# A sixth weight buffer, receptance written in place, and the first unit's small products spread among dense steps

## The chip, the cores and the metric

The kernel runs on one core of one Trainium2 chip. The metric is the device time of one execution in microseconds. It was timed three times before the change: 1114.33, 1113.28 and 1114.30, median 1114.3.

## The reference, cut to what matters

The model has two layers, batch 1, 256 positions, width 2048, all in 32-bit floats. The first layer is an RWKV-7 mixer, the second a sparse attention mixer; only the first is touched here. Its core, cut:

```python
rkvz = jnp.einsum('nbtd,nde->nbte', mixed[:4], w_rkvz)        # four 2048 x 2048 products
decay = jnp.exp(-jnp.exp(w_log))
a = jax.nn.sigmoid(a0 + (xa @ a1) @ a2)
kk = heads(k * k_k); kk = kk / max(norm(kk), 1e-12)
k = k * (1.0 + (a - 1.0) * k_a)
o = wkv7_scan(r, decay, k, v, -kk, kk * a)                      # 32 heads of 64
o = group_norm(o) * ln_g + ln_b
bonus = jnp.sum(r * k * r_k, axis=-1, keepdims=True) * v
y = ((o + bonus) * jax.nn.silu(z)) @ w_o
```

The scan updates a 64 x 64 state per head and position: `S = S*w + (S a) b + v k`, and reads `o = S r`.

## The kernel before, in words

**Dense products.** Every weight is read once from memory in raw pieces of [128, 1024] floats by the SP queue (class `Weights`, `load`, L172). ScalarE copies a unit of a piece to a rounded high part (`whi`, L207), VectorE subtracts to get the low part (`wlo`, L192). TensorE then makes three matmuls where one would do: high by high, high by low, low by high. Raw buffers are five (`RAWB`), units are split three ahead of use (`AHEAD`). `ensure` (L194) asks for the piece that lies as many pieces on as there are raw buffers each time it splits a unit.

**Stages.** The value rows come first, then z and k columns in turn (`stage_k`, L715, works out decay, normalised keys and the rest for each block of 128 columns and stores them as `sp` in memory, `spd`). A triangular inverse for each chunk of 64 positions is worked out on VectorE (`stage_t`, L810), for the first half of the heads early, for the second half during the scan. The scan works in chunks of 64 positions, four of them, and in eight units of four heads (two column blocks `x`, two heads `h` each).

**The scan.** From there on the order on every engine is written out by hand (`in_order`). The receptance columns of unit U+1 and later the output product are a stream of dense steps, each of three matmuls of 256 columns (`pair_block`, L1248; L1257 to L1259), which `fill(n)` (L1273) places n at a time between the small matmuls of the scan. After each dense step `sch.pump()` lets the background work (`stage_t`) put its next instruction into VectorE's program. Preparing a unit has these steps in `prep` (L1049): `G` and `Y` complete the inverse, `B0`, `B1` transpose, `A0`, `A1` make the receptance-key products (each 48 matmuls of 64 x 64 on four chunks), `M0` to `M2` mask them on VectorE. `scale_r` (L1031) multiplies the receptance by the decay into `ar` and makes `mb`, the receptance times the bonus keys. Unit 0 is prepared by the list `PROLOGUE`, later units by `AUX`, a table of steps by phase.

A unit then runs twelve phases (`phase`, L1107): for each of four chunks a removal (`L1105`), a solve (`L1128`) and an output and state update (`L1134`, `L1137`). Phase number v is 3 times the chunk plus the step. In phase 0 the 32 matmuls of the bonus sums (`L1116`) come first. `FILL` gives the number of dense steps behind each phase: 32 a unit, as many as a unit of receptance has. The prologue has 16 of them.

`SPL` holds a unit's `sp`: keys and their inverse-decayed partner (512 columns), decays (260), bonus keys `kr` (256), decayed negative keys `at` (256), and behind these 256 more for the receptance that `scale_r` writes.

Of the kernel before, what the change touches and what calls it, by code (L numbers as in the profile page):

```python
# [71 lines left out]
KLAG = 2  # L72
AUX = {2: ("B0",), 3: ("G",), 4: ("B1", "Y"), 7: ("A0",), 9: ("A1",), 10: ("T", "M2"), 11: ("M0", "M1")}
NORM = {0: ("s0", "s1"), 1: ("s2", "s3", "rg"), 2: ("v",), 3: ("b",), 4: ("nmr",), 5: ("02", "24"), 6: ("46",), 7: ("68",), 8: ("g", "+", "z")}
FILLL = (3, 4, 4, 0, 0, 5, 4, 0, 4, 0, 4, 4)
PROLOGUE = ("R0", "R1", 6, "G", "B0", 4, "I", "Y", "B1", 2, "A0", 2, "A1", "M2", "M0", "M1", "V5", 2)
ZHOOK = 9
PACES, PACE, HOLD = (0.0, 1.8, 0.9, 0.9), [0.0], [False]
FILL = (3, 4, 4, 0, 0, 5, 4, 0, 4, 0, 4, 4)
FILLO, LASTFILL = 4, 36  # L80
QZ = (0, 25, 24, 1, 2, 23, 22, 21, 3, 20, 19, 18, 4, 17, 16, 15, 14, 13, 12, 11, 10)
# [63 lines left out]
class Weights:  # L145


    def __init__(self, tc, pool, raw_bufs, ahead):
        self.tc = tc
        self.nc, self.pool, self.raw_bufs, self.ahead = tc.nc, pool, raw_bufs, ahead  # L150
        self.pieces, self.order, self.loads, self.raw, self.hl = [], [], [], {}, []
        self.loaded = self.split = self.taken = 0
        self.on_pool = set()
        self.kept_from, self.kept_pool = math.inf, None
        self.due, self.late, self.hold = [], False, False

    def add(self, ap, per, queue=True):
# [14 lines left out]
    def load(self, n):  # L172
        while self.loaded < min(n, len(self.loads)):
            p = self.loads[self.loaded]
            ap, per = self.pieces[p]
            n_, cols = ap.shape[1:]
            t = self.raw_pool.tile([128, 1024], F32, name="wraw", bufs=self.raw_bufs)
            v = t[:, :n_ * cols].rearrange("p (k c) -> p k c", k=n_)
            self.nc.sync.dma_start(v, ap)
            self.raw[p] = [v, n_ // per]  # L180
            self.loaded += 1
# [12 lines left out]
    def ensure(self, n):  # L194
        while self.split < min(n, len(self.order)):
            p, u = self.order[self.split]
            if not self.hold:
                self.low()
            self.load(self.loads.index(p) + self.raw_bufs)
            ap, per = self.pieces[p]  # L200
# [18 lines left out]
def hybrid_kernel(ctx: ExitStack, tc: tile.TileContext, a: dict, out: bass.AP):  # L219
# [475 lines left out]
    ph0.release()  # L695
    banks(acc=(2, 0, 1), la=(3,), rn=(4, 7), ab=(5, 6))
    late = tc.alloc_tile_pool(name="late", bufs=1, side="right")
    kph = tc.alloc_tile_pool(name="kph", bufs=1)
# [16 lines left out]
    def stage_k(j):  # L715
# [16 lines left out]
        ksb = tmp("ksb")  # L732
        sqk = tmp("t1")
        S.activation(ksb, pk, AF.Copy)
# [16 lines left out]
        yield 1000.0  # L751
        rnx = tmp("rnx")
        S.activation(rnx.rearrange("p (a b n) -> p a b n", a=2, b=2),
# [12 lines left out]
        yield 800.0  # L766
        nk = tmp("nk")
        V.scalar_tensor_tensor(nk, ksb, KKN[:, j:j + 1], rn[:, :256], op0=OP.mult, op1=OP.mult)
# [166 lines left out]
    def phase_z3():  # L935
        nonlocal A10, T00, vt, zt
        ps = two()
        for k in range(NK):
            yield from rows_step(ps, "z", k, W.get(), 512)
            used.add(("z", k))  # L940
            if k == ZHOOK:
                sch.require(lambda: len(a1done) == 16)
                kph.release()
                early = tc.alloc_tile_pool(name="early", bufs=1, side="right", reuse_waits="tile")
                early_pool.append(early)
                one = lambda name, shape: early.tile(shape, F32, name=name)
                SPL0.extend(one(f"spl0{x}", [128, SPW + 256]) for x in range(2))
# [28 lines left out]
    one = lambda name, shape: scan.tile(shape, F32, name=name)  # L976
    SPL = [SPL0, [one(f"spl1{x}", [128, SPW + 256]) for x in range(2)]]
    Yb.append(one("Yb1", [128, 2, NCH, 64]))
# [45 lines left out]
    def parts(U, x):  # L1024
# [3 lines left out]
                t[:, SPW - 512:SPW - 256],  # L1028
                t[:, SPW - 256:].rearrange("p (x c t) -> p x c t", x=2, c=NCH))

    def scale_r(U, x):  # L1031
# [3 lines left out]
        pr = rps[U % 2][:, 256 * x:256 * x + 256]  # L1035
        V.tensor_tensor(ar[:, 1], c3(pr), pp[:, :, 1:], op=OP.mult)
        V.tensor_tensor(mb[:, x], pr, kr, op=OP.mult)
        G.tensor_copy(PCH[U][:, x], pp[:, :, CH])

# [9 lines left out]
    def prep(step, U):  # L1049
# [19 lines left out]
        elif step[0] == "B":  # L1069
# [6 lines left out]
            sch.t += 300  # L1076
        elif step[0] == "A":
            x = int(step[1])
            if x == 0:
                AT[U] = (pair_tile(2), rps[U % 2])  # L1080
            both, m = AT[U]
            BK, pp, kr, ar = parts(U, x)
            for c in range(NCH):
                o = x * 256 + c * 64
                for e in range(2):
                    for h in range(2):
                        k = h ^ e
                        PE.matmul(both[R[k], h * 512 + o:h * 512 + o + 64], BK[R[h], c, k, :], ar[R[h], 1, c, :], start=True, **mm)
                for h in range(2):
                    PE.matmul(m[R[h], o:o + 64], BK[R[h], c, h, :], ar[R[h], 0, c, :], start=True, **mm)  # L1090
            sch.t += 900
        else:
# [14 lines left out]
    def phase(U, c, p):  # L1107
        uv, px, pu, pS = UV[U % 2], view(U, 0, 64), view(U, 64, 64), view(U, 128, 64)
        O = view(U, 192 + 64 * c, 64)
        st = SST[U][0] if c else None  # L1110
        if p == 0:
            if c == 0:
                for i in range(NCH):
                    for x, h in each:
                        o = x * 512 + 448 + 2 * i
                        PE.matmul(PBK[U][H(x, h), o:o + 2], mb[R[h], x, 64 * i:64 * i + 64], ones2[R[h]], start=True, **mm)  # L1116
            removal(U, c)
            if c:
                for k, o in enumerate((px, O)):
                    for x, h in each:  # L1120
                        PE.matmul(o[H(x, h), x], ARS[U % 2][x][R[h], k, c - 1, :], st[R[h], x, :], start=False, **mm)
            X = scan.tile([128, 2, 64], F32, name="X", bufs=2)
# [139 lines left out]
    def stream():  # L1262
        for u in range(NU):
            yield from pair_block("r", rps[u % 2])
        phase_done.add("r")
        banks(acc=(0, 1))
        for nb, k0, k1 in OSEQ:
# [48 lines left out]
    for U in range(NU):  # L1316
# [3 lines left out]
        for v in range(12):  # L1320
# [23 lines left out]
            if v == 6 and U + 1 < NU:  # L1344
                scale_r(U + 1, 0)
                scale_r(U + 1, 1)
            for step in AUX.get(v, ()):
                if step == "T":
                    if U:
                        turn_y(P)  # L1350
                elif U + 1 < NU:
                    prep(step, U + 1)
            if U:
# [15 lines left out]
            if v == 10:  # L1369
                load_rows(vt, vd, U)  # L1370
                load_rows(zt, zd, U)
            fill(FILLO if U + 1 == NU else FILLL[v] if U + 2 == NU else FILL[v])
            sch.pump()
# [22 lines left out]
    def open_kv():  # L1396
        nonlocal bp, kvp, xlp, ssh, rsh
        scan.release()
        early_pool[0].release()
        late.release()  # L1400
        bp = ctx.enter_context(tc.tile_pool(name="bp", bufs=1, side="right"))
        kvp = tc.alloc_tile_pool(name="kvp", bufs=1)
# [513 lines left out]
```

## Time and profile before

| what | value |
|---|---|
| median of three timed runs | 1114.3 us |
| the profiled execution's own time | 1114.21 us |
| its span on the profile page | 1112.4 us |
| mean granted TensorE clock | 0.995 |
| TensorE busy | 1091.2 us, 98% |
| VectorE, ScalarE, GpSimd busy | 836.1, 737.7, 329.6 us |
| read from memory, written to it | 200.49 MB, 22.58 MB |

In the profile PE is TensorE's matmuls, PEld its weight loads, DVE is VectorE, ACT ScalarE, POOL GpSimd, SP the engine that issues most transfers. Times are microseconds from the start of the span. A row of waits gives the engine and line that waited, what ended the wait, the total, the count and the longest. A row of the timeline gives start, duration, engine, line, operation, tiles, count, and in brackets idle time ahead of it and what ended it; "issue" means that the profile shows nothing that it waited for. The prologue of the scan begins near 350.7 us with its first dense step, unit 0's phases near 361, unit 1's at 387.67.

### The profile page before, as it was taken

The page shows a single profiled execution, that of the slowest core. Times are in us where ns is not written, and L with a number is a line of the kernel's source. Part 1 is how long each engine was busy: PE and PEld are TensorE (multiplying, and loading weights), DVE is VectorE, ACT ScalarE, POOL GpSimd, SP SyncE. Part 2 cuts the span into 40 slices and gives each one's busy share as a digit, 9 for nine tenths or more (in the row PEclk, how much of TensorE's full clock was granted, in tenths as well). Part 3 has the DMA queues.
Part 4 walks back from the last instruction along what each step waited for, and adds up shares of the span by engine and source line. Part 5 has one row for each costly group of instructions (what it writes and reads, how often), then busy time and mean ns, then how long its engine had stood idle before and what let it go on. Part 6 is the DMA issues. An engine that isn't in the chain of part 4 may idle for free.

```text
span 1112.4 us, 25288 instructions
## 1 busy us (share of the span) xinstructions
PE 1091.2 (98%) x9232; PEld 957.1 (86%) x9232; DVE 836.1 (75%) x1784; ACT 737.7 (66%) x1779; POOL 329.6 (30%) x409
## 2 busy tenths in 40 slices
PE   8999999999999999999999999999999999999997
PEld 7788899898889888999888888788989999988887
DVE  6999976779887796666667876665677988886564
ACT  7767877676775467776557766665666677775553
POOL 1300035424448456652200110100323324432012
PEclk9999999999999999999999999999999999999999
DMA  7458978877879777865578668675745354735762
GB/s 260 152 194 235 248 212 249 247 197 216 260 222 269 223 194 211 245 197 156 160 250 277 197 203 260 195 253 169 198 139 152 101 145 131 187 103 194 281 199 100
DMA packets 221965, 224.74 MB, mean 202 GB/s; under 512 B 48368, under 2 KB 173392, under 8 KB 221456
## 3 DMA queue, kind: packets, MB, share of 16 engines
q1 hardware_dynamic: 216512, 217.60, 66.1%
q0 software_dynamic: 4864, 4.92, 1.6%
q8 instruction: 73, 1.20, 0.4%
q10 hardware_dynamic: 464, 0.59, 0.1%
q14 instruction: 52, 0.43, 0.1%
HBM read 200.49 MB, written 22.58 MB: 201 GB/s over the span
## 4 chain that ended last, share of the span: by engine, by line
PE 54%; DVE 4%; DMA 2%; issue 1%; ACT 1%; POOL 0%; POOLq 0%; DVEq 0%; ACTq 0%
PE bank L619 9%; PE bank L617 9%; PE bank L616 9%; PE bank L1657 5%; PE bank L235 4%; PE bank L1658 3%; DVE wlo L192 2%; PE bank L1257 1%; PE pair L619 1%; PE pair L616 1%; PE pair L617 1%; PE bank L1258 1%; PE bank L1259 1%; PE bank L1223 1%; PE pair L1134 1%
## 5 line engine op out<-in xcount | busy, mean ns | idle before, releaser
L192 DVE TENSOR_TENSOR wlo<-wraw,whi 128x512 fp32r<-128x512 f32 (+2 forms) x616 | 440.3, 728 | 144.0 <-ACT whi L207 139.7
L207 ACT ACTIVATE whi<-wraw 128x512 fp32r<-128x512 f32 (+2 forms) x664 | 401.8, 618 | 179.5 <-PE bank L619 69.6
L192 POOL TENSOR_TENSOR wlo<-wraw,whi 128x512 fp32r<-128x512 f32 (+2 forms) x48 | 61.4, 1279 | 174.3 <-ACT whi L207 134.9
L617 PE MATMUL bank<-wlo,mh 128*128 128x512 f32 (+1 forms) x288 | 109.4, 381 | 0.8 <-DVE wlo L192 0.7
L617 PE MATMUL bank<-wlo,mhl 128*128 128x512 f32 (+2 forms) x288 | 107.9, 375 | 0.0
L619 PE MATMUL bank<-whi,ml 128*128 128x512 f32 (+1 forms) x288 | 107.9, 379 | 0.0
L619 PE MATMUL bank<-whi,mhl 128*128 128x512 f32 (+2 forms) x288 | 107.3, 373 | 0.0
L616 PE MATMUL bank<-whi,mhl 128*128 128x512 f32 (+2 forms) x288 | 99.5, 373 | 0.3 <-ACT Vt L1539 0.3
L616 PE MATMUL bank<-whi,mh 128*128 128x512 f32 (+1 forms) x288 | 92.0, 381 | 0.3 <-ACT whi L207 0.2
L1657 PE MATMUL bank<-mhl,whi 128*128 128x512 f32 x256 | 91.9, 397 | 0.0
L1257 PE MATMUL bank<-mhl,whi 128*128 128x256 f32 x256 | 78.6, 307 | 2.0 <-issue 2.0
L617 PE MATMUL bank<-wlo,kvh 128*128 128x512 f32 x192 | 76.0, 396 | 0.0
L634 PE MATMUL bank<-mh,whi 128*128 128x256 f32 x256 | 75.2, 294 | 0.4 <-ACT whi L207 0.4
L619 PE MATMUL bank<-whi,kvl 128*128 128x512 f32 x192 | 75.3, 392 | 0.0
L636 PE MATMUL bank<-mh,wlo 128*128 128x256 f32 x256 | 73.7, 290 | 0.0
L635 PE MATMUL bank<-ml,whi 128*128 128x256 f32 x256 | 73.4, 287 | 0.0
L1658 PE MATMUL bank<-mhl,wlo 128*128 128x256 f32 x256 | 73.0, 285 | 0.3 <-DVE wlo L192 0.3
L1259 PE MATMUL bank<-mhl,wlo 128*128 128x256 f32 x256 | 72.7, 284 | 0.1
L1258 PE MATMUL bank<-mhl,whi 128*128 128x256 f32 x256 | 72.7, 284 | 0.0
L616 PE MATMUL bank<-whi,kvh 128*128 128x512 f32 x192 | 66.7, 391 | 0.0
L617 PEld LDWEIGHTS bank<-wlo,mh 128*128 128x128 f32 x288 | 54.1, 188 | 11.5 <-DVE wlo L192 2.0
L619 PEld LDWEIGHTS bank<-whi,ml 128*128 128x128 f32 x288 | 54.2, 188 | 9.6
(384 smaller groups left out, 2746.4 us busy)
## 6 DMA issues: line engine op xcount, KB each, us to landing
wraw<-in_a_w_rkvz_dram SPq DMA_DIRECT2D x128, 512.0 KB, 5.1
wraw<-in_kv_w_dram SPq DMA_DIRECT2D x48, 512.0 KB, 4.4
wraw<-in_b_w_in_dram SPq DMA_DIRECT2D x40, 512.0 KB, 4.3
wraw<-in_a_w_o_dram SPq DMA_DIRECT2D x32, 512.0 KB, 4.9
wraw<-in_b_w_o_dram SPq DMA_DIRECT2D x32, 512.0 KB, 3.7
spd<-sp SPq DMA_DIRECT2D x16, 642.0 KB, 4.7
wraw<-in_b_w_in_dram SPq DMA_DIRECT2D x24, 384.0 KB, 3.2
wraw<-in_cmp_w_dram SPq DMA_DIRECT2D x16, 512.0 KB, 3.9
```

What stands on the lines that cost most here:

```text
L192: eng.tensor_tensor(lv, src, hv.bitcast(F32), op=OP.subtract)
L207: self.nc.scalar.activation(hv, src, AF.Copy)
L616: PE.matmul(o, mh[:, ts], wh[:, 0, :], start=k == ends[0], stop=False)
L617: PE.matmul(o, mh[:, ts], wl[:, 0, :], start=False, stop=False)
L619: PE.matmul(o, ml[:, ts], wh[:, 0, :], start=False, stop=k == ends[1])
L634: PE.matmul(o, wh[:, s, :], mh, start=k == 0 and first, stop=False, **kw)
L636: PE.matmul(o, wl[:, s, :], mh, start=False, stop=k == NK - 1, **kw)
L1257: PE.matmul(oo, wh[:, i, c], mh, start=k == 0 and x == 0, stop=False, **kw)
L1258: PE.matmul(oo, wh[:, i, c], ml, start=False, stop=False, **kw)
L1259: PE.matmul(oo, wl[:, i, c], mh, start=False, stop=k == NK - 1, **kw)
L1657: PE.matmul(o, wh[:, s, :], beside[("u", k)], start=k == 0, stop=False)
L1658: PE.matmul(o[:, :T], wl[:, s, :], mh, start=False, stop=k == NK - 1)
```

## The change: what it does

- From the end of the value stage to the end of the receptance stream the raw pieces go through six buffers, not five; the sixth is a pool of its own (`spare`). `t1`, `rnx` and `nk` of `stage_k` go from two buffers to one, and the `SPL` tiles lose their last 256 columns.
- The receptance is therefore written over the bonus keys: `scale_r` makes `mb` first and then `ar[:, 0]` in the place of `kr`. The two rows of `ar` have changed places, and all that reads them is turned accordingly.
- `A0` and `A1` now make chunks 0 and 1 alone; new steps `a0` and `a1` make chunks 2 and 3. For unit 0 (prologue) and for unit 1 (prepared in unit 0's phases, new table `AUX0`) there are dense steps between the halves. For later units the halves follow each other as before.
- The prologue's 16 dense steps and unit 0's 32 are dealt out anew (`PROLOGUE`, `FILL0` and the numbers in `AUX0`); their sums are the same. The inverse of the second half of the heads may start (`I`) after seven dense steps, not ten.
- Unit 0's bonus sums move from phase 0 to phase 5.

```diff
-AUX = {2: ("B0",), 3: ("G",), 4: ("B1", "Y"), 7: ("A0",), 9: ("A1",), 10: ("T", "M2"), 11: ("M0", "M1")}
+AUX = {2: ("B0",), 3: ("G",), 4: ("B1", "Y"), 7: ("A0","a0"), 9: ("A1","a1"), 10: ("T", "M2"), 11: ("M0", "M1")}
-PROLOGUE = ("R0", "R1", 6, "G", "B0", 4, "I", "Y", "B1", 2, "A0", 2, "A1", "M2", "M0", "M1", "V5", 2)
+PROLOGUE = ("R0", "R1", 3, "G", 2, "B0", 2, "I", "Y", "B1", 2, "A0", 1, "a0", 2, "A1", 2, "a1", "M2", "M0", "M1", "V5", 2)
 FILL = (3, 4, 4, 0, 0, 5, 4, 0, 4, 0, 4, 4)
+FILL0 = (3, 4, 4, 0, 0, 5, 5, 0, 5, 0, 2, 2)
+AUX0 = {2: ("B0",), 3: ("G",), 4: ("B1", "Y"), 7: ("A0", 1, "a0"), 9: ("A1", 1, "a1"), 10: ("M2",), 11: ("M0", "M1")}
...
+            if self.spare is not None and (self.loaded - self.spare_from) % (self.raw_bufs + 1) == 0:
+                t = self.spare.tile([128, 1024], F32, name="wspare", bufs=1)
+                self.spare_last = self.loaded
+            else:
+                t = self.raw_pool.tile([128, 1024], F32, name="wraw", bufs=self.raw_bufs)
...
-            self.load(self.loads.index(p) + self.raw_bufs)
+            n0 = self.loads.index(p)
+            self.load(n0 + self.raw_bufs + (self.spare is not None or n0 <= self.spare_last))
...
-        sqk = tmp("t1")
+        sqk = tmp("t1", 1)
...
-                t[:, SPW - 256:].rearrange("p (x c t) -> p x c t", x=2, c=NCH))
+                t[:, SPW - 512:].rearrange("p (x c t) -> p x c t", x=2, c=NCH))
...
-        V.tensor_tensor(ar[:, 1], c3(pr), pp[:, :, 1:], op=OP.mult)
         V.tensor_tensor(mb[:, x], pr, kr, op=OP.mult)
+        V.tensor_tensor(ar[:, 0], c3(pr), pp[:, :, 1:], op=OP.mult)
...
-        elif step[0] == "A":
+        elif step[0] in "Aa":
             x = int(step[1])
-            if x == 0:
+            if step == "A0":
                 AT[U] = (pair_tile(2), rps[U % 2])
...
-            for c in range(NCH):
+            for c in range(NCH // 2) if step[0] == "A" else range(NCH // 2, NCH):
...
+        if (c, p) == ((0, 0) if U else (1, 2)):
+            for i in range(NCH):
+                for x, h in each:
+                    o = x * 512 + 448 + 2 * i
+                    PE.matmul(PBK[U][H(x, h), o:o + 2], mb[R[h], x, 64 * i:64 * i + 64], ones2[R[h]], start=U > 0, **mm)
         if p == 0:
-            if c == 0:
-                for i in range(NCH):
-                    for x, h in each:
-                        o = x * 512 + 448 + 2 * i
-                        PE.matmul(PBK[U][H(x, h), o:o + 2], mb[R[h], x, 64 * i:64 * i + 64], ones2[R[h]], start=True, **mm)
...
-            for step in AUX.get(v, ()):
+            for step in (AUX if U else AUX0).get(v, ()):
...
+                    if isinstance(step, int):
+                        fill(step)
+                    else:
+                        prep(step, U + 1)
...
-            fill(FILLO if U + 1 == NU else FILLL[v] if U + 2 == NU else FILL[v])
+            fill(FILL0[v] if U == 0 else FILLO if U + 1 == NU else FILLL[v] if U + 2 == NU else FILL[v])
```

More of the change, by code (lines that the diff above doesn't have):

```diff
@@ L155, in __init__ @@
         self.due, self.late, self.hold = [], False, False
+        self.spare, self.spare_from, self.spare_last = None, 0, -1
     def add(self, ap, per, queue=True):
@@ L176, in load @@
             n_, cols = ap.shape[1:]
-            t = self.raw_pool.tile([128, 1024], F32, name="wraw", bufs=self.raw_bufs)
+            if self.spare is not None and (self.loaded - self.spare_from) % (self.raw_bufs + 1) == 0:
[3 more added lines that the diff above has]
+                t = self.raw_pool.tile([128, 1024], F32, name="wraw", bufs=self.raw_bufs)
             v = t[:, :n_ * cols].rearrange("p (k c) -> p k c", k=n_)
@@ L696, in hybrid_kernel @@
     banks(acc=(2, 0, 1), la=(3,), rn=(4, 7), ab=(5, 6))
+    spare = tc.alloc_tile_pool(name="spare", bufs=1, side="right")
+    W.spare, W.spare_from = spare, W.loaded
     late = tc.alloc_tile_pool(name="late", bufs=1, side="right")
@@ L751, in stage_k @@
         yield 1000.0
-        rnx = tmp("rnx")
+        rnx = tmp("rnx", 1)
         S.activation(rnx.rearrange("p (a b n) -> p a b n", a=2, b=2),
@@ L766, in stage_k @@
         yield 800.0
-        nk = tmp("nk")
+        nk = tmp("nk", 1)
         V.scalar_tensor_tensor(nk, ksb, KKN[:, j:j + 1], rn[:, :256], op0=OP.mult, op1=OP.mult)
@@ L946, in phase_z3 @@
                 one = lambda name, shape: early.tile(shape, F32, name=name)
-                SPL0.extend(one(f"spl0{x}", [128, SPW + 256]) for x in range(2))
+                SPL0.extend(one(f"spl0{x}", [128, SPW]) for x in range(2))
                 A10 = one("a10", [128, 2, NCH, 64])
@@ L976, in hybrid_kernel @@
     one = lambda name, shape: scan.tile(shape, F32, name=name)
-    SPL = [SPL0, [one(f"spl1{x}", [128, SPW + 256]) for x in range(2)]]
+    SPL = [SPL0, [one(f"spl1{x}", [128, SPW]) for x in range(2)]]
     Yb.append(one("Yb1", [128, 2, NCH, 64]))
@@ L1087, in prep @@
                         k = h ^ e
-                        PE.matmul(both[R[k], h * 512 + o:h * 512 + o + 64], BK[R[h], c, k, :], ar[R[h], 1, c, :], start=True, **mm)
+                        PE.matmul(both[R[k], h * 512 + o:h * 512 + o + 64], BK[R[h], c, k, :], ar[R[h], 0, c, :], start=True, **mm)
                 for h in range(2):
-                    PE.matmul(m[R[h], o:o + 64], BK[R[h], c, h, :], ar[R[h], 0, c, :], start=True, **mm)
-            sch.t += 900
+                    PE.matmul(m[R[h], o:o + 64], BK[R[h], c, h, :], ar[R[h], 1, c, :], start=True, **mm)
+            sch.t += 450
         else:
@@ L1120, in phase @@
                     for x, h in each:
-                        PE.matmul(o[H(x, h), x], ARS[U % 2][x][R[h], k, c - 1, :], st[R[h], x, :], start=False, **mm)
+                        PE.matmul(o[H(x, h), x], ARS[U % 2][x][R[h], 1 - k, c - 1, :], st[R[h], x, :], start=False, **mm)
             X = scan.tile([128, 2, 64], F32, name="X", bufs=2)
@@ L1265, in stream @@
         phase_done.add("r")
+        W.spare = None
         banks(acc=(0, 1))
@@ L1351, in hybrid_kernel @@
                 elif U + 1 < NU:
-                    prep(step, U + 1)
+                    if isinstance(step, int):
+                        fill(step)
+                    else:
+                        prep(step, U + 1)
             if U:
@@ L1400, in open_kv @@
         late.release()
+        spare.release()
         bp = ctx.enter_context(tc.tile_pool(name="bp", bufs=1, side="right"))
```

## The prediction

> **What bounds the kernel now.** I read the page's busy shares first, then what TensorE (PE) waited for, then PE's timeline around its longest gap, then windows and DMA answers there.
>
> ```profile
> PE 1091.2 (98%) x9232; PEld 957.1 (86%) x9232; DVE 836.1 (75%) x1784; ACT 737.7 (66%) x1779; POOL 329.6 (30%) x409
> q8 instruction: 73, 1.20, 0.4%
> ```
>
> PE is busy 98% of the span. A change that moves work on other engines is worth only the PE time that those engines hold up. The second row is a DMA queue that carries instructions: 1.20 MB in 73 packets. PE has 9232 matmuls and 9232 weight loads, and 18464 / 73 = 253, so the packets look like PE's own program in blocks of about 250 instructions (an estimate from these rows). The longest rows of PE's waits:
>
> ```profile
> PE bank L784 <- POOL sp L775: 2.1, 4, 0.7
> PE bank L1257 <- issue: 2.0, 1, 2.0
> ...
> PE bank L1090 <- issue: 0.7, 1, 0.7
> ```
>
> L1257 is a dense receptance step and L1090 the last product of a receptance-key group; the change touches both. "Issue" means that no data was late. PE's timeline shows the places:
>
> ```profile
> 362.00 0.19 PEld L1257 LDWEIGHTS bank<-mhl,whi 128*128 128x128 f32 x1
> ...
> 364.10 0.37 PE L1257 MATMUL bank<-mhl,whi 128*128 128x256 f32 x1 [2.02 <-issue]
> ...
> 383.75 0.21 PE L1090 MATMUL bank<-spl 64*64 64x64 f32 x1 [0.67 <-issue]
> ```
>
> At 362.0 a weight load has been done and its matmul comes 2.1 us later. Windows around it (columns: window, length, then busy time and count of PE, weight loads, DVE, ACT, POOL, PE clock, DMA share, GB/s):
>
> ```profile
> 357.35:362.05 4.70, 4.70 (x149) 4.23 (x149) 1.58 (x3) 0.93 (x2) 3.05 (x6) 1.00 1.06 348
> 362.05:364.10 2.05, 0.03 (x4) 0.14 (x2) 1.84 (x11) 0.80 (x2) 0.72 (x1) 1.00 1.06 296
> 364.10:367.52 3.42, 3.42 (x21) 3.08 (x21) 3.18 (x13) 0.77 (x3) 2.04 (x3) 0.50 1.12 309
> 367.52:382.90 15.38, 15.38 (x362) 14.07 (x361) 10.53 (x40) 8.62 (x26) 4.67 (x10) 1.00 0.79 223
> 362.05:382.90 20.85, 18.82 (x384) 17.29 (x382) 15.55 (x62) 10.18 (x30) 7.43 (x14) 0.92 0.87 244
> ```
>
> Three things are to be seen. The DMA engines are saturated (1.06) before and in the gap. After the gap PE has half its clock for 3.42 us, which loses 1.71 us. From the first gap to the second there are 384 + 382 = 766 counted instructions, three blocks of about 253 plus a few semaphore instructions. So both gaps sit on a block boundary. The instruction queue's row in the stretches 353.0 to 354.6, 361.3 to 362.7, 368.4 to 369.9 and 381.0 to 382.3, with the data queue's row of the stretch between the first two, in which no instruction row appears for this queue:
>
> ```profile
> q8 instruction: 1, 0.02, 5.3%
> q1 hardware_dynamic: 1143, 2.03, 101.3%
> q8 instruction: 1, 0.02, 5.6%
> q8 instruction: 1, 0.02, 5.4%
> q8 instruction: 1, 0.02, 5.5%
> ```
>
> The block of 361.3 to 362.7 is followed by PE's restart at 364.10, that of 381.0 to 382.3 by the restart at 383.75: 1.4 us behind the transfer each time. My reading: PE holds about two blocks, asks for the next when it enters the last one it has, and ran dry. The 298 instructions of the 4.70 us window are about one block and the forty or so that wait in PE's queue, so the request was made near 357.35, found the rings full, moved after 361.3 and was usable at 364.10: 6.75 us. The next request, at 364.1, moved by 369.9 and by the same 1.4 us was usable at 371.3: 7.2 us. PE ran through its block in 4.7 us because it was nearly all tiny matmuls.
>
> [...]
>
> **The change, part by part.** *Four groups and the bonus sums.* A group of 48 products becomes two of 24 with dense steps between, and 32 bonus matmuls leave the place just ahead of the gap for the sixth of the unit's twelve phases (phase 5, counted from 0). A dense step is six instructions in 0.355 us (three starts 0.118 apart, rows below); 32 bonus matmuls are 64 instructions in 0.48 us (387.67 to 388.15).
>
> ```profile
> 358.94 0.28 PE L1258 MATMUL bank<-mhl,whi 128*128 128x256 f32 x1
> 359.06 0.28 PE L1259 MATMUL bank<-mhl,wlo 128*128 128x256 f32 x1
> 359.27 0.34 PE L1088 MATMUL pair<-spl 64*64 64x64 f32 x8
> ...
> 360.14 0.28 PE L1090 MATMUL bank<-spl 64*64 64x64 f32 x4
> 360.35 0.39 PE L1257 MATMUL bank<-mhl,whi 128*128 128x256 f32 x1
> ...
> 387.67 0.64 PE L1116 MATMUL pair<-ones,mb 64*64 64x2 f32 x32
> 388.15 0.32 PE L1105 MATMUL pair<-uv,ama 64*64 64x64 f32 x8
> ```
>
> With 64 instructions gone from ahead of it, the boundary of 362.05 falls 64 instructions further on in the old order. Behind the gap stood three dense steps (18), a group of 16, four dense steps (24) and a few semaphores, so it now falls on the start of L1134 of phase 2. A run of n dense steps takes n x 0.355 + 0.21 with its change-over; 24 products take 24 x 0.02 + 0.13 = 0.6 (44 of them in 0.87, and 0.13 of change-over, worked out below), and a group of eight such matmuls 0.29 (estimates). From the request to that point PE does: the rest of one half group (0.3), one dense step (0.56), a half (0.6), two steps (0.92), a half (0.6), two (0.92), a half (0.6), two (0.92), removal (0.29), three (1.27), L1128 (0.29) and four (1.63), together 8.9 us, against a latency of 6.75 to 7.2. This block comes in time, with about 2 us to spare. **Gain: 2.02 + 1.71 = 3.7 us.** In phases 7 to 9 the block of 383.75 was 0.67 late. There the change puts two single steps (0.56 each) into the groups and a fifth step (0.36) into phase 8, taken from phases 10 and 11: 1.5 us more ahead of that boundary. Gain 0.67, together 4.4.
>
> *What splitting costs.* From the last dense start to a tiny one are 0.21 us (359.06 to 359.27) where 0.118 is the pace, and back 0.21 (360.14 to 360.35) where four tiny ones at the group's pace (44 in 0.87) take 0.08. One more change of kind each way is 0.09 + 0.13 = 0.22, and up to 0.33 if the pipeline drains at both ends (0.21 and 0.13). There are eight dense runs in the prologue for five, and two more splits in unit 0's phases: 5 x 0.33 = 1.6 us, lower bound 1.1. I take 1.6, since the dense runs between are one or two steps.
>
> *What comes late next.* The bonus sums now follow a run of phases 3 and 4 with no dense step. The next boundary, 256 instructions after the first, falls at the end of L1064 of phase 4, because all between is unchanged. That stretch runs from L1134 at 368.58 to 373.42 before:
>
> ```profile
> 368.58:373.42 4.84, 4.84 (x132) 4.33 (x131) 2.72 (x11) 2.88 (x9) 0.56 (x1) 1.00 0.95 295
> ```
>
> The request is made some 37 instructions ahead (L1128 and four dense steps, 1.8 us), so the block has 4.84 + 1.8 = 6.6 us. At 6.75 to 7.2 us it is 0.15 to 0.6 late. The lower bound is 0, if the rings are emptier. For the upper one, the request that became usable at 371.3 may have been made before the gap, 37 instructions ahead of it, at 361.5: then the latency is 9.8 us and the block 3.2 late. I take 0.5, near the first reading, since PE had not yet got the block it would have to enter.
>
> *Sixth raw buffer.* ScalarE waited for late weights in this stretch:
>
> ```profile
> 352.93 0.63 ACT L207 ACTIVATE whi<-wraw 128x512 fp32r<-128x512 f32 x1 [2.92 <-DMA wraw<-in_a_w_rkvz_dram]
> ```
>
> PE lost nothing by it: the split weights are three units (twelve dense steps) ahead. The buffer takes the wait away and so keeps the copies of the prologue (L1057, L1075), now three dense steps earlier, from queuing behind a late weight. The SP queue issues as many loads as before, each at the same release, one piece further on: no added traffic. 0 us, and 0.6 if the cover were gone (one split late).
>
> *Receptance in place, smaller tiles, single buffers.* The two products of `scale_r` change places on DVE (0.41 us each) and nothing waits within that; the reload of the overwritten key columns now waits for the last reader of the receptance, which the next piece waited for already. `t1`, `rnx` and `nk` are each read at once after being written: 0, and up to 16 columns x 0.1 us if a copy came to wait. Stage T's start moves three dense steps ahead, into DVE's idle time:
>
> ```profile
> 360.47 0.69 DVE L1096 TENSOR_TENSOR ama<-bank,cst 128x512 f32<-128x512 f32 x1 [3.25 <-PE bank L1090]
> ```
>
> **Sum:** -4.4 + 1.6 + 0.5 = -2.3 us. The profiled execution took 1114.21 us (span 1112.4), 0.1 below the median of 1114.3, so the forecast is **1111.9 us**.
>
> [...]
>
> ```profile
> 244.65:248.06 3.41, 2.10 (x27) 1.69 (x26) 3.41 (x10) 1.29 (x4) 2.50 (x3) 1.00 0.49 158
> 248.06:251.48 3.42, 3.42 (x14) 3.24 (x15) 3.31 (x8) 2.99 (x8) 2.66 (x3) 0.50 0.92 296
> ```
>
> **The rivals.** *The late block moves* (slower). If the fetch at the end of phase 4 waits longer than 6.6 us, the gap returns there: at 9.8 us it is 3.2 us idle and 1.7 of half clock, 4.9 in place of the 0.5 taken, 1116.3; if the following block, asked for only then, is 0.7 late too, 1117. It decides from about 1.3 us of idle, where the clock falls. For it: DMA share 1.12 just then. Against: both latencies seen were under 7.3.
>
> *The gap isn't a fetch.* Then it stays, the splits cost 1.6, and the time is 1115.8. For it: no row ties the packet to the stall. Against: 766 instructions between the gaps and 1.4 us twice. [...]
>
> *The gain is given back.* The inverse of the second half of the heads ends on DVE, then goes through two DMAs to PE:
>
> ```profile
> 424.42 5.54 DMA tnd<-invT
> ...
> 436.96 5.59 DMA Yb<-yvd
> ```
>
> In PE's waits stands:
>
> ```profile
> PE pair L1055 <- DMA Yb<-yvd: 0.3, 1, 0.3
> ```
>
> PE already waits 0.3 us for it at 442. If DVE does not start that chain earlier, all of 2.3 is waited there: 1114.2. Against: DVE had 3.25 us idle at 360.47 alone, in the stretch that shrinks, and gets the inverse's first steps there.
>
> *The key phase is rescheduled.* The single buffers could add or remove stalls such as those at L784 and the half clock of 248.06 (1.3 + 1.7 = 3.0 us): 1109 or 1115.
>
> **How the numbers follow.** A run set of this kernel tells 0.2% (2.2 us) from no change, so faster is below 1112.1, slower above 1116.5. Chances: forecast 0.56 (its own range 1110.8 to 1113.2), late block 0.12, no fetch 0.08, given back 0.10, key phase 0.14 (half each way). Faster: 0.43 of the forecast's 0.56, 0.07 of the key phase: 0.50. Slower: most of the late block, 0.09. Same: 0.41. The range 1109.0 to 1115.9 takes in the key phase both ways, the give-back and the case without a fetch, and leaves out the late block.
>
> **What would show it.** Right: no "issue" wait over 1 us on PE between 350 and 390, clock 1.00 there, the first bonus group of unit 1 about 2 to 3 us before 387.67, no weight wait on ScalarE. Residue: an "issue" gap at or just behind L1064 of phase 4. Wrong: a gap at the same instruction count with the clock at 0.50, or PE waiting over 2 us at L1055 near 440.

## The result and the profile after

The changed kernel takes **1120.1 us** (five runs, 1119.3 to 1121.4) against 1114.3 (1113.3 to 1115.1): a ratio of 1.0057, with an interval of 1.0046 to 1.0068. It is 5.8 to 6.4 us slower, where 1111.9 was forecast. The profiled execution took 1119.68 us, its span is 1117.8. The five runs had a mean granted clock of 0.994, the runs of the kernel before beside the experiments 0.996; by that some 2 of the 6 us are clock and the rest are waits (an estimate).

The page's busy shares and the queue of instructions, after:

```profile
PE 1094.0 (98%) x9232; PEld 958.3 (86%) x9232; DVE 838.1 (75%) x1784; ACT 736.6 (66%) x1779; POOL 329.7 (29%) x409
q8 instruction: 73, 1.20, 0.5%
```

The work is the same, instruction for instruction in number. What PE waited for between 345 and 450 us:

```profile
PE pair L1115 <- DVE ama L1106: 1.4, 1, 1.4
PE pair L1138 <- ACT X L1133: 1.1, 2, 0.7
PE pair L1115 <- DVE S L1150: 1.1, 1, 1.1
PE pair L1144 <- ACT uv L1140: 0.7, 1, 0.7
PE bank L1269 <- DVE wlo L199: 0.5, 1, 0.5
```

Both "issue" gaps of before (2.0 and 0.7 us) are gone, as forecast. In their place PE waits for VectorE five lines down: masks (`ama`), low parts (`wlo`), state copies (`S`), and what ScalarE makes of them (`X`, `uv`; lines stand some ten further down than before). Behind these waits the clock falls for twice as long as before, 6.83 us against 3.42 (windows; columns as in the prediction):

```profile
364.50:376.10 11.60, 7.89 (x135) 6.67 (x133) 10.77 (x42) 3.78 (x11) 3.34 (x5) 1.00 1.06 322
376.10:382.93 6.83, 6.83 (x105) 6.33 (x98) 2.21 (x8) 2.89 (x8) 4.10 (x9) 0.50 0.77 213
```

In the first window VectorE is busy 10.77 of 11.60 us. Its timeline shows why it is behind, after and (second fence) before:

```profile
362.82 0.18 DVE L840 COPY invT<-invA 128x16 f32<-128x16 f32 x1 [3.52 <-DMA invA<-abdd]
...
364.19 0.69 DVE L199 TENSOR_TENSOR wlo<-wraw,whi 128x512 fp32r<-128x512 f32 x1
...
365.47 0.69 DVE L1106 TENSOR_TENSOR ama<-bank,cst 128x512 f32<-128x512 f32 x1
```

```profile
355.99 0.18 DVE L830 COPY invT<-invA 128x16 f32<-128x16 f32 x1 [0.44 <-DMA invA<-abdd]
```

The first copy of the second inverse stands in VectorE's program and waits there for `invA` until 362.8, and for these 3.52 us nothing else runs on VectorE: the masks that PE needs for its first removal come only at 365.47. Before, the same copy waited 0.44 us and VectorE was then free from 357.2 to 360.5. SP's queue shows why the data is late, after and before:

```profile
343.23 1.77 SPq L806 DMA_DIRECT2D abdd<-abs  x4
348.65 0.82 SPq L1008 DMA_DIRECT2D spl<-spd  x2
349.56 0.39 SPq L186 DMA_DIRECT2D wraw<-in_a_w_rkvz_dram  x1
350.06 2.61 SPq L942 DMA_DIRECT2D Yb<-yvd  x4
352.71 1.29 SPq L829 DMA_DIRECT2D invA<-abdd  x2
```

```profile
340.48 1.77 SPq L796 DMA_DIRECT2D abdd<-abs  x4
342.35 0.87 SPq L998 DMA_DIRECT2D spl<-spd  x2
...
346.61 1.16 SPq L819 DMA_DIRECT2D invA<-abdd  x2
```

SP issues the load of unit 0's keys (`spl`) right behind the stores out of `abs` before, and 3.7 us behind them after. What it waited for there, between 339 and 352 us:

```profile
SPq L1008 <- DMA abdd<-abs: 3.5, 2, 3.2
```

This wait is new. The smaller `SPL` tiles and the sixth buffer moved the pool that holds unit 0's keys down by 2 KB a partition, onto the second buffer of `abs` (169664 to 170688; `spl00` was at 171936, now at 169888). The keys may not be loaded until the last stores have read `abs`, and everything on SP stands behind. Of the 6 us by which the inverse's data is asked for later (352.71 against 346.61), 2.75 were there before that wait, at the stores themselves.

To compare kernels I use one stretch of equal work, from the first receptance step of unit 0 to the first bonus product of unit 1 (starts of these matmuls in the trace). Before it begins at 339.24 and takes 48.43 us, with 3.41 us at half clock; after it begins at 341.99 and takes 52.62, with 6.83 at half clock. So 2.75 us are lost ahead of it and 4.19 in it. Unit 1 loses 0.85 more (24.00 against 23.15); of the 7.8 us, 2.4 are back by the end of the span.

Matched matmul by matmul, PE of the changed kernel is 1.3 us behind from 180 us on (its clock was at half from 178.13 to 181.54), 3.1 behind at 230 (it waits 1.6 us there for a low part), 1.3 behind at 253 (the kernel before had half clock from 248.06, the changed one had not), and 2.7 behind at 300. So the falls of the clock ahead of the stretch cancel, and the waits do not. The 2.4 us come back mostly where the kernel before waits and the changed one doesn't: 0.53 for `X` at 430.74 of the kernel before, 0.33 for `Yb` at 442.59, 0.64 for a high part at 723.32, 0.34 for a low part at 915.10.

### The profile page after: what moved, and what is told of

Read it like the earlier page. It is cut to its first block, busy times and chain, and to the rows that moved or that the text cites. A ratio compares the mean times of both kernels' runs of the same rounds, so it can differ in the third digit from the quotient of the medians.

```text
span 1117.8 us, 25312 instructions
## 1 busy us (share of the span) xinstructions
PE 1094.0 (98%) x9232; PEld 958.3 (86%) x9232; DVE 838.1 (75%) x1784; ACT 736.6 (66%) x1779; POOL 329.7 (29%) x409
## 4 chain that ended last, share of the span: by engine, by line
PE 58%; DVE 3%; ACT 1%; issue 1%; POOLq 0%; POOL 0%; DVEq 0%; ACTq 0%
PE bank L624 9%; PE bank L625 9%; PE bank L627 9%; PE bank L1672 5%; PE bank L243 5%; PE bank L1673 3%; PE bank L1267 2%; PE pair L627 1%; PE pair L624 1%; PE bank L1268 1%; DVE wlo L199 1%; PE bank L1269 1%; PE pair L625 1%; PE bank L1233 1%; PE pair L1144 1%
## 5 line engine op out<-in xcount | busy, mean ns | idle before, releaser
L199 DVE TENSOR_TENSOR wlo<-wraw,whi 128x512 fp32r<-128x512 f32 (+2 forms) x582 | 413.9, 725 | 136.7 <-ACT whi L215 133.3
L215 ACT ACTIVATE whi<-wraw 128x512 fp32r<-128x512 f32 (+2 forms) x630 | 380.5, 618 | 172.7 <-PE bank L627 66.0
```

The source lines that it names most:

```text
L199: eng.tensor_tensor(lv, src, hv.bitcast(F32), op=OP.subtract)
L215: self.nc.scalar.activation(hv, src, AF.Copy)
```

## The experiments

Ratios are to the kernel before on the same chip; 0.0010 is 1.1 us.

| run | what it is | ratio, interval | stretch, half clock in it |
|---|---|---|---|
| changed kernel | | 1.0057, 1.0046 to 1.0068 | 52.62, 6.8 |
| e1_order | new order alone | 1.0035, 1.0021 to 1.0050 | 51.09, 6.8 |
| e2_memory | new layout, old order | 1.0013, 0.9999 to 1.0027 | 47.42, 0 |
| e3_abs_first | changed, `abs` out of the way | 1.0040, 1.0025 to 1.0054 | 52.00, 10.2 |
| e4_single | before, three single buffers | 1.0007, 0.9993 to 1.0021 | 46.03, 0 |
| e5_late_start | changed, inverse after ten steps | 1.0027, 1.0017 to 1.0038 | 47.30, 0 |
| e6_early_start | before, inverse after seven | 1.0014, 1.0000 to 1.0029 | 46.28, 0 |
| e7_order_late | new order, inverse after ten | 1.0014, 1.0003 to 1.0025 | 47.28, 0 |
| e8_abs_late | e3 and e5 together | 1.0022, 1.0011 to 1.0033 | 50.21, 6.8 |
| e9_order_end | new order, inverse after sixteen | 1.0075, 1.0059 to 1.0090 | 47.51, 0 |
| e10_bonus | before, bonus sums moved | 1.0003, 0.9989 to 1.0017 | 47.86, 3.4 |
| e11_memory_abs | e2, `abs` out of the way | 1.0017, 1.0005 to 1.0028 | 48.07, 3.4 |
| e12_bonus_late | e10, inverse after fourteen | 1.0072, 1.0055 to 1.0089 | 47.84, 3.4 |
| e13_spare_late | e11, sixth buffer used later | 1.0008, 0.9997 to 1.0019 | 47.54, 0 |
| e14_bonus_pool3 | e10, three low parts on GpSimd | 1.0035, 1.0019 to 1.0050 | 51.20, 10.2 |
| e15_bonus_pool8 | e10, eight low parts on GpSimd | 1.0054, 1.0037 to 1.0070 | 52.13, 6.8 |
| e16_pool3 | before, three low parts on GpSimd | 1.0017, 1.0006 to 1.0028 | 47.15, 3.4 |
| e17_all_back | changed, three causes taken back | 1.0000, 0.9989 to 1.0012 | 47.31, 0 |
| e18_bonus_early | e10, inverse dealt out otherwise | 0.9998, 0.9985 to 1.0012 | 46.43, 0 |

### Which part of the change

The new order alone takes the lists, the halves and the move of the bonus sums into the kernel before; the new layout alone is the changed kernel with the old lists:

```diff
-PROLOGUE = ("R0", "R1", 3, "G", 2, "B0", 2, "I", "Y", "B1", 2, "A0", 1, "a0", 2, "A1", 2, "a1", ...
+PROLOGUE = ("R0", "R1", 6, "G", "B0", 4, "I", "Y", "B1", 2, "A0", "a0", 2, "A1", "a1", ...
...
-        if (c, p) == ((0, 0) if U else (1, 2)):
+        if (c, p) == (0, 0):
...
```

> The kernel before with the new order alone: groups in halves, dense steps dealt out anew, the inverse allowed to start three dense steps earlier, unit 0's bonus sums in phase 5. No sixth buffer, receptance not in place, old double buffers, so all addresses are those of before. Theory A (the order helps as forecast, and the loss comes from the layout, which makes SP's load of unit 0's keys wait for the last key block's stores): 1112 us, no issue gap over 1 us on PE, clock 1.00 from 350 to 390. Rival (the order itself blocks VectorE, since the inverse starts earlier than its data, or the splits cost more): 1117 to 1120, with clock 0.50 near 376.

> The changed kernel with the old order: whole groups, old dealing of dense steps, inverse start after ten dense steps, bonus sums of unit 0 in phase 0. Sixth buffer, receptance in place and single buffers stay. Theory A: SP's wait of 3.5 us stays and the loads for the inverse land some 6 us later than in the kernel before, so the time stays well above the kernel before: 1116 to 1120. Rival (order to blame): 1114 to 1115.

In e3 two tiles are asked for first, so that `abs` lies at 144992; e4 is the three `bufs=1` alone:

```diff
     kph = tc.alloc_tile_pool(name="kph", bufs=1)
+    for _ in range(2):
+        kph.tile([128, T], F32, name="abs", bufs=2)
```

> The changed kernel with one difference: the two buffers from which the last key block's stores read (abs) are given the lowest addresses of the key stage, so that they no longer lie where unit 0's keys are loaded. Nothing else in order or traffic is different. Theory A: no wait of SP at the first key load, loads of the inverse land 3.5 us or more sooner, no half clock near 376, time 1113 to 1116 (what the key phase lost, 1.3 to 2.7 us, stays). Rival (the sixth buffer's loads crowd the rings, or the order is to blame): 1119 to 1120, unchanged.

> The kernel before with t1, rnx and nk in one buffer instead of two, nothing else. If the 1.3 to 2.7 us that the changed kernel is behind by the end of the key phase come from the single buffers: 1115.5 to 1117, with PE stalls at the key stage's squares and transposes. If they come from the sixth buffer: 1114.3.

My theory put the blame on the layout, and fell: the order alone is 3.9 us slower, at its old addresses, and the layout with the old order only 1.4. The overlap is real, since in e3 SP's wait is gone. The ratio is 1.9 us better, but the two intervals overlap, and most of the loss stays. The single buffers alone show no loss. In e1 `invA` is asked for 0.8 us later than before (347.42 against 346.61) and lands 2.9 later (358.75 against 355.89), and the copy still blocks VectorE for 3.12 us; PE waits and the clock falls:

```profile
358.84 0.18 DVE L832 COPY invT<-invA 128x16 f32<-128x16 f32 x1 [3.12 <-DMA invA<-abdd]
```

```profile
372.70:379.52 6.82, 6.82 (x103) 6.36 (x98) 2.17 (x8) 2.90 (x8) 4.11 (x9) 0.50 0.71 192
```

### The earlier start of the inverse

```diff
-... 2, "I", "Y", "B1", 2, "A0", 1, "a0", 2, ...
+... 2, "Y", "B1", 2, "A0", 1, "I", "a0", 2, ...
```

for e5, e7 (with the order alone) and e8 (with `abs` moved); in e6 `"B0", 4, "I"` of the kernel before becomes `"B0", 1, "I", 3`.

> The changed kernel, but the inverse of the second half of the heads may start after ten dense steps of the prologue, as before, not after seven. Theory C (the earlier start puts the inverse's first copy, which waits for its data, and then its small steps on VectorE ahead of the splits, masks and state copies that PE needs): 1114 to 1116, no clock of 0.50 near 376, VectorE's wait at the inverse's first copy under 1.5 us. Rival E (the splits and the new dealing of the dense steps cost it): 1119 to 1120, unchanged.

> The kernel before with the inverse's start after seven dense steps, not ten; nothing else, and the order of the dense steps and the small products on PE is that of before. Theory C: VectorE waits some 3 us at the inverse's first copy, the splits and state copies behind it come late, 1117 to 1119. Rival E: 1114, no change.

> The new order alone (groups in halves, dense steps dealt out anew, bonus sums of unit 0 in phase 5, all addresses and buffers as before), with the inverse's start after ten dense steps. Theory C with the instruction blocks as forecast: 1111 to 1112.5, no issue gap over 1 us and clock 1.00 from 350 to 390. Rival E: 1118, as the new order was with the early start. A third reading (the gap of before was rest for VectorE, which is the next bound there): 1114 to 1115, with PE waiting for wlo and S near 370.

> The changed kernel with both: inverse's start after ten dense steps, and the abs buffers at the lowest addresses of the key stage, clear of unit 0's keys. If the late start and the address wait are two separate losses: 1112 to 1114, 1 to 2 us below the changed kernel with the late start alone. If the address wait costs nothing: equal to that one.

The start after ten steps takes 3.3 us off the changed kernel and 2.3 off the order alone; the stretch falls from 52.6 to 47.3 and from 51.1 to 47.3. The early start in the kernel before costs 1.6 (0 to 3.2), less than expected: its `invA` lands at 356.73, and the copy waits 1.44 us.

In e5's trace unit 0's phases end where they did before (387.81 against 387.67), and the loss that is left lies behind them: unit 1 takes 26.57 us, not 23.15. PE's wait there and the clock after it:

```profile
PE bank L1269 <- issue: 1.6, 1, 1.6
```

```profile
412.35:419.18 6.83, 6.83 (x72) 6.14 (x71) 5.47 (x20) 2.41 (x7) 1.71 (x1) 0.50 0.53 130
```

This is a gap for instructions at 410.49, one of the kind that the change was to remove, at a place that it does not touch.

The third reading of e7 came nearest, with waits for `S` and `X` and none for `wlo`. In e7 PE has no gap for instructions in the prologue and phase 0, no half clock, and a stretch 1.15 us shorter. It is no shorter than that, for PE now waits in chunk 1:

```profile
369.06 0.34 PE L1107 MATMUL pair<-uv,ama 64*64 64x64 f32 x8 [0.99 <-DVE S L1142]
370.78 0.34 PE L1130 MATMUL pair<-X,Yb 64*64 64x64 f32 x8 [0.65 <-ACT X L1125]
```

Unit 1 then takes 24.65 us, not 23.15 (PE waits 0.65 for `mb` at 401.25 and has a gap of 0.45 for instructions at 408.33), and nothing of the gain is left. In e8 the move of `abs` gives 0.6 us more, which is inside the interval.

### Where the gain of the order went

e10 is the kernel before with the condition `((0, 0) if U else (1, 2))` for the bonus sums; e12 is e10 with `"I"` after fourteen steps, e9 is e7 with `"I"` last.

> The new order alone with old addresses and buffers, as in the run of the order with the late start, but the inverse may start only after all sixteen dense steps of the prologue. Theory D (with the instruction gap gone, VectorE's backlog of inverse steps is what PE waits for: 1.0 us for the state copy and 0.6 for X near 368 in the run with the start after ten): those waits vanish, the stretch from the first receptance step to unit 1's first bonus group falls from 47.3 to 45.5 or so, and 1 to 2 us come back as a wait at the heads' second inverse (L1057) near 442, so 1113 to 1115. Rival (the waits for the state copy have another cause): they stay, and so does the stretch of 47.3.

> The kernel before with one edit: unit 0's 32 bonus products go from phase 0 to phase 5. No halves, no new dealing, the inverse's start as before. The block theory of the forecast: 64 fewer instructions ahead of the old gap put the block's end at the start of phase 2's output products, some 3.6 us of work further on for 2.2 us less of latency, so the gap of 2.0 us at the first removal is gone or under 0.5. Gap not a fetch: it stays at the removal of phase 0 at 1.8 to 2.1 us. By theory D a wait for VectorE's state copy of up to 1 us takes its place. Time 1112.5 to 1114.5.

> The kernel before with unit 0's bonus products in phase 5 and the inverse's start after fourteen dense steps, not ten. Theory D: the state copies are in time, the gap is gone, and the inverse of the second half of the heads ends about 1 us later: 1112 to 1113.5, the best of the lot, unless PE waits for it at 442 (then 1114).

The gap at the first removal (2.02 us before) is gone in e10 by that one move. What remains is at L1064 in phase 4, where the forecast had put it: 0.47 us from the start of the product before it, 0.25 of them idle.

```profile
369.50 0.34 PE L1105 MATMUL pair<-uv,ama 64*64 64x64 f32 x8 [0.98 <-DVE S L1140]
371.22 0.34 PE L1128 MATMUL pair<-X,Yb 64*64 64x64 f32 x8 [0.61 <-ACT X L1123]
372.88 0.19 PE L1064 MATMUL pair<-gs,t 64*64 64x32 f32 x1 [0.25 <-issue]
```

Counted in PE's recorded instructions, the two gaps of before stand at number 5057 and 5825, the one of e10 at 5313, others in e5, e7, e9, e16 and e18 at 6849 (weight loads and semaphore instructions counted, the first instruction behind the gap taken). They lie 256, 512 and 1024 apart, and the instruction queue moved 1.20 MB in 73 packets for 18654 recorded instructions of PE in the kernel before, about 256 a packet. So I read them as ends of instruction blocks; the move only changed which work stands there. And PE waits 1.0 us for the state copy, which stands on VectorE behind 22 small steps of the inverse and two low parts (363.51 to 369.16). With a later start that wait is gone, in e9 and e12, and the price is paid elsewhere. PE's waits in e12, and ScalarE's row behind the first:

```profile
PE pair L1128 <- ACT X L1123: 6.4, 2, 6.0
PE pair L1064 <- issue: 2.0, 1, 2.0
```

```profile
434.21 2.22 ACT L898 ACTIVATE invA<-invT 128x256 f32<-128x256 f32 x4 [5.87 <-DVE invT L873]
```

ScalarE's program holds the turning of the finished inverse at a fixed place, and stood there for 5.87 us with the next `X` behind it. I had looked for that limit at L1055 near 442 and expected 1 to 2 us; it lies at 431 and costs 6, and the clock after it.

### The sixth buffer

e11 is e2 with `abs` moved; e13 lets the sixth buffer begin late:

```diff
-    W.spare, W.spare_from = spare, W.loaded
...
             if k == ZHOOK:
+                W.spare, W.spare_from = spare, W.loaded
```

> The changed kernel with the whole old order (as in the run of the new memory layout with the old order) and the abs buffers clear of unit 0's keys. Sixth buffer, receptance in place and single buffers are what is left of the change. If the address was the only cost of the layout: 1113 to 1114, SP's first key load right behind the last stores. If the sixth buffer costs by itself: 1115 to 1116, with the wait for wlo near 230 of 1.5 to 2.5 us as in all runs that have it.

> The sixth buffer, the receptance in place, the single buffers and the clear abs buffers with the old order, but the sixth buffer is used only from the last quarter of the z and k columns on, after the first inverse has its data. Theory F (the sixth buffer lets a weight load run ahead of the last stores that the inverse's loads wait for; VectorE's first inverse copy then blocks the splits, 7.5 us near 231 against 4.5 us in the kernel before, and PE waits up to 3.0 us for wlo): that copy's wait is back to about 4.5 us, PE's gap near 230 under 1.5 us, time 1113.5 to 1114.8. Rival (layout or single buffers cost it): gap of 1.6 to 3.0 us and 1116 as without the delay.

With the old order and without the overlap the layout still costs 1.9 us. SP's queue of e11 and of the kernel before, ahead of the first inverse:

```profile
217.94 0.39 SPq L186 DMA_DIRECT2D wraw<-in_a_w_rkvz_dram  x1
218.42 1.16 SPq L186 DMA_DIRECT2D wspare<-in_a_w_rkvz_dram  x1
219.67 3.48 SPq L808 DMA_DIRECT2D abdd<-abs  x4
226.86 1.14 SPq L831 DMA_DIRECT2D invA<-abdd  x2
```

```profile
215.22 2.88 SPq L179 DMA_DIRECT2D wraw<-in_a_w_rkvz_dram  x2
218.83 1.92 SPq L796 DMA_DIRECT2D abdd<-abs  x4
223.75 1.14 SPq L819 DMA_DIRECT2D invA<-abdd  x2
```

The extra weight load of 512 KB is issued ahead of the last four stores; their issue takes 3.48 us, not 1.92, and the first inverse's data is asked for 3.1 us later (0.5 of it e11 was behind already). VectorE's first copy of that inverse then blocks the low parts, and PE waits for `wlo` (VectorE's and PE's row of e11, then of e13):

```profile
231.77 0.18 DVE L842 COPY invT<-invA 128x16 f32<-128x16 f32 x1 [7.46 <-DMA invA<-abdd]
```

```profile
232.83 0.39 PE L644 MATMUL bank<-mh,wlo 128*128 128x256 f32 x1 [2.73 <-DVE wlo L199]
```

```profile
229.83 0.18 DVE L841 COPY invT<-invA 128x16 f32<-128x16 f32 x1 [5.41 <-DMA invA<-abdd]
```

```profile
230.90 0.39 PE L644 MATMUL bank<-mh,wlo 128*128 128x256 f32 x1 [0.68 <-DVE wlo L199]
```

One trace each would not do here, since VectorE's wait varies from execution to execution: it is 6.1 to 7.5 us, mean 6.6, in the six traces with the sixth buffer from the start, and 4.5 to 6.2, mean 5.2, in the fourteen without it or with the late one. So it is 1.4 us longer on average, and PE's wait for the low part grows by as much: 1.35 to 2.73 us, mean 1.84, in the six, and 0 to 1.42, mean 0.45, in the fourteen. This is the same trap as at 362, one stage earlier. The time follows from e11 to e13, by 1.0 us, which is inside the intervals.

### Low parts on GpSimd

```diff
+    W.on_pool.update(range(W.split, W.split + 3))
     for U in range(NU):
```

with 3 (e14, e16) or 8 (e15).

> The kernel before with unit 0's bonus products in phase 5, and the next three low parts (wlo) of unit 0's phases made by GpSimd, not VectorE. Theory D (VectorE's backlog of inverse steps, splits and masks is the bound from 361 to 372 once the instruction gap is gone): two low parts of 0.68 us leave the queue ahead of the state copy, so PE's wait for it (1.0 us) and some of that for X goes: 1112 to 1113.5. Rival (a low part on GpSimd at 1.3 us is late itself, or GpSimd's transfers are held up by it): PE waits for wlo, 1114.5 to 1117.

> As the run with three low parts on GpSimd, but eight, that is all of unit 0's. Theory D: VectorE has 5.4 us less to do before unit 1, the second inverse ends earlier and PE's waits for it near 442 (0.8 us with the bonus move alone) go too: 1111.5 to 1113. Rival: as there, 1115 to 1118, since GpSimd issues the transfers of the next unit's inverse blocks.

> The kernel before with the first three low parts of unit 0's phases on GpSimd, nothing else. Theory D: VectorE is not the bound while PE has its instruction gap of 2 us there, so 1114, no change (half a microsecond either way). If GpSimd's low parts are late: 1115 to 1117.

All are slower, e14 and e15 by more than their rivals had it, and by another cause: GpSimd's low parts come in time, but two of VectorE's own steps beside them get longer, 0.18 to 1.16 us and 0.23 to 1.27 (last section), and in e14 PE waits 1.4 us for the next low part that VectorE makes.

### Closing the account

e17 joins e5, e3 and e13. In e18 the inverse starts after seven steps in e10, and `"V5"` (five steps of it in a row behind the masks) becomes `"V2"`.

> The changed kernel with the three suspected losses taken back: the inverse's start after ten dense steps, the sixth buffer in use only after the first inverse has its data, the abs buffers clear of unit 0's keys. What is left is the new order and the layout. If the three are the whole loss beyond the order itself: 1114.5 to 1116, as the new order alone with the late start (ratio 1.0014 to the kernel before). If something else of the layout costs: over 1116.5.

> The kernel before with unit 0's bonus products in phase 5, and the inverse's steps dealt out otherwise on VectorE: the start after seven dense steps, not ten, and in return two, not five, steps in a row right behind the masks. Six of the inverse's small steps leave the stretch between the masks and the first state copy. Theory D: PE's wait for the state copy falls from 1.0 us by some 0.8, that for X likewise, no later end of the inverse: 1112 to 1113.5. Rival (the earlier start meets the late data of the inverse, and the clock gate takes the rest): 1115 to 1117.

e17 is level with the kernel before: from 1.0057 by the later start to 1.0027, by `abs` to 1.0022, by the late sixth buffer to 1.0000. The middle step alone can't be told from nothing. Some of being level is the clock: e17's runs had a mean of 0.998, those of the kernel before beside them 0.997, about 1.6 us (an estimate from the unrounded means, 0.9981 and 0.9967). In e18 the wait for the state copy is gone, as theory D has it, but PE comes earlier to the block end, 5.47 us behind the start of L1134 of phase 2 against 6.70 in e10, and its gap grows from 0.25 us to 0.84:

```profile
372.06 0.34 PE L1128 MATMUL pair<-X,Yb 64*64 64x64 f32 x8 [0.50 <-ACT X L1123]
374.31 0.19 PE L1064 MATMUL pair<-gs,t 64*64 64x32 f32 x1 [0.84 <-issue]
```

Its stretch is 46.43 us, the shortest with the moved sums, and its time no different. No version beat the kernel before.

## Why the prediction was wrong

- **The instruction gaps** (-4.4): the places were right. They are gone, and e10 shows the next gap where it was put, with 0.47 us against 0.5. How many blocks PE holds, when it asks for the next and the forty instructions in its queue were my estimate; no run shows them. The size was luck: the same block end has 0.84 us of idle in e18 and 2.04 in e12, where the clock fell behind it for 3.4 us, as the rival of the late block has it. The term was too large: its 1.71 us of half clock is not sure. Of six traces with a gap of 1.6 us or more at the first removal, the clock fell in three (before, e11, e16), for 3.4 us each, and held at 1.00 in three (e4, e6, e13), the last after 1.96 us of "issue" (last section). The 1.3 us of idle from which the rival of the late block has it fall came from one place (244.65 to 248.06); in e11 the clock held behind 1.67 us of idle (228.36 to 231.77).
- **Splits** (+1.6 for five): the three in the prologue cost 0.71. From `scale_r`'s first product to the first scan product it took 10.26 us before (351.00 to 361.26), 10.97 in e7 (351.07 to 362.04). That is 0.24 each, 1.2 for five.
- **"Stage T's start moves three dense steps ahead, into DVE's idle time"** (0): this is the step that failed worst, by 2.3 us (e1 against e7) to 3.3 (the changed kernel against e5). I took the 3.25 us at 360.47 as free, and did not ask when the data of the moved instruction lands: `invA` landed at 355.9 in the kernel before, 0.44 us after the copy was ready for it. Moved ahead, the copy waits, and this closes the free time to all that stands behind: in the changed kernel nothing ran on VectorE between 359.31 and 362.82.
- **"The SP queue issues as many loads as before, each at the same release, one piece further on: no added traffic"** (0): it failed at "one piece further on". The load goes ahead of stores on which VectorE's next instruction depends; some 1 to 2.5 us (e11 against e13, inside the intervals, and e8 against e17), with PE's wait at 230 longer by 1.4 on average.
- **Receptance in place, smaller tiles, single buffers** (0): instructions and single buffers were rightly costed at nothing. I did not ask what the tiles come to lie on: the new addresses made SP wait 3.5 us, which costs at most about 1.9 us with the early start (e3, inside the intervals) and nothing measurable with the old order (e11 against e2).
- **The rival "the gain is given back"** had 0.10 and described e7, e10 and e17, though at the wrong place: not at L1055 near 442 (0.4 us in e7), but at the state copy and `X` of chunk 1, 1.6 us together in e7 and in e10. The gap in which PE stood had been VectorE's time to work off its inverse: it was busy 1.84 of the 2.05 us. So even without the three losses the forecast gain of 2.3 us isn't there.
- **No weight wait on ScalarE, first bonus group of unit 1 earlier**: the first came true (between 338 and 372 us ScalarE waits for no transfer of weights, where it was 3.3 us before), and the forecast had put it at nothing. The group came at 394.61, not 2 to 3 us before 387.67.

What stays open: the 1.4 us that the changed kernel loses between 253 and 300 us, which may be chance (e18, whose order there is that of before, began the stretch at 342.54, after half clock from 7.25 to 14.08), and why e5 meets the block end at 410 with a gap of 1.62 us, where e7 and e9 have about 0.5 and e17 none.

## What to carry to other kernels

Idle time on an engine that keeps to its program's order, as VectorE did here behind the waiting copy for 3.52 us, is free only for an instruction whose operands have already landed: before one is moved ahead, look up when its data arrives and what stands behind it. A deeper prefetch on a queue shared with small transfers isn't free either, since it can delay those that come after it (here four stores took 3.48 us to issue, not 1.92), and a smaller tile may slide onto one that a late transfer still reads (here SP waited 3.5 us for it). When a stall is removed from the bounding engine, look at what the others did in that time.

## What the runs showed that I had not expected

In e14 two steps of VectorE took about 1.0 us longer while a low part ran on GpSimd. GpSimd's rows, then VectorE's, and last the same two steps of VectorE in e10:

```profile
364.64 1.31 POOL L192 TENSOR_TENSOR wlo<-wraw,whi 128x512 fp32r<-128x512 f32 x1 [1.37 <-ACT whi L207]
366.46 1.27 POOL L192 TENSOR_TENSOR wlo<-wraw,whi 128x512 fp32r<-128x512 f32 x1 [0.51 <-ACT whi L207]
```

```profile
364.83 1.16 DVE L860 COPY invT<-invM 128x32 f32<-128x32 f32 x1
...
366.54 1.27 DVE L849 TENSOR_TENSOR invX<-invA,invT 128x64 f32<-128x64 f32 x1
```

```profile
364.05 0.18 DVE L860 COPY invT<-invM 128x32 f32<-128x32 f32 x1
...
364.79 0.23 DVE L849 TENSOR_TENSOR invX<-invA,invT 128x64 f32<-128x64 f32 x1
```

In e10 that copy takes 0.18 us and that product 0.23. In e14 each begins just after one on GpSimd and ends with it, at 365.99 and 367.81 against 365.95 and 367.73; in e16 two others take 1.18 and 1.33. So the 0.68 us saved cost about 1.0. What ties the two engines together there, no run shows.

The clock's answer to a gap of 2 us (it fell to 0.50 after 2.02 in the kernel before and held at 1.00 after 1.96 in e13) seems to depend on where the gap lies. In each trace with several half-speed stretches, these begin whole multiples of 3.4133 us apart (kernel before: 248.06, 364.11 and 1108.22, which is 34 and 218 of them, 860.16 us in all; changed kernel: 178.13, 376.11 and 1113.38, which is 58 and 216), and but for the last, at the end of the execution, they last 3.41 or a multiple of it (6.83, 10.24). Cut on this grid, the three traces whose clock fell have the whole gap at the first removal in one cell, with PE busy 1.39, 1.72 and 1.84 us of its 3.41 (before, e11, e16). In the three whose clock held, a cell's edge splits the gap, and the emptier cell has 1.99, 2.11 and 2.36 (e13, e6, e4). That the place decides is read from six traces, not shown by a run made for it, and PE's busy share alone does not decide: elsewhere the clock fell behind cells with 2.10 (kernel before, from 244.65) and 2.55 (e10, from 370.17), and held behind one with 1.74 (e11, from 228.36). From trace to trace the edges lie elsewhere: counted from the start of the span the first is at 2.30 us in the kernel before, 1.36 in e6 and 3.09 in e11.
